# Three-block sequence model on one core: 64-row products set apart, PSUM groups copied out by ScalarE before rotation, and other moves in the order of work

## The chip, the core and the metric

The kernel runs on one core of one Trainium2 chip. The time is that of one execution on the device, in microseconds (us); lower is better. The core has five engines that run side by side and wait for one another through semaphores: TensorE (PE in the profile, with its weight loads as PEld), VectorE (DVE), ScalarE (ACT), GpSimd (POOL) and SyncE (SP), which here issues the transfers. PE writes its results to PSUM, which has eight banks of 128 rows by 512 fp32 numbers; everything else lives in SBUF.

## The reference

A sequence of 2048 tokens with 1024 channels passes through three blocks, four layers in all. Every layer projects its input with a wide matrix, mixes along the sequence in two or three branches, gates each branch, and projects back. The parts that the change touches are these:

```
# layer 1: HGRN, 4 heads of 128, chunks of 64 (beside it: sliding-window attention with rotated q and k)
G = cumsum(log_f);  q_dec = q*exp(G);  k_dec = k*exp(-G)
A = tril(q_dec @ k_dec^T)
o = A @ v + q_dec @ S_prev
S = exp(G_last)*S_prev + (k*exp(G_last-G))^T @ v

# layers 2 (gated linear attention) and 3 (retention): 4 heads, 64 key rows and 128 value columns each
scores = causal_or_decay(q @ k^T)
o = scores @ v + q @ s_in           # s_in: state entering the chunk
# layer 3: q and k are rotated first
rot(x) = concat(x1*cos - x2*sin, x1*sin + x2*cos)

# layer 4: mLSTM, 4 heads of 128; gates from two columns per head
i_pre = h @ w_i + b_i;  lf = log_sigmoid(h @ w_f + b_f)
b = cumsum(lf);  m = running max of (b_t - b_s + i_s);  decays and weights from exp of these
# every layer
mix = branch * silu(gate);   out = mix @ w_out
```

All inputs are fp32, and so is the output.

## The kernel before

The 2048 tokens are worked in four blocks of 512 (`TB`). `run` takes the blocks in pairs and goes through the layers pair by pair: layer 1 for blocks 0 and 1, layer 2 for blocks 0 and 1, and so on to layer 4, then the same for blocks 2 and 3. So each layer stands four times in the program.

**Projections.** Each fp32 operand is split into a rounded high part and the rest: `ah` and `al` for the activations, `whi` and `wlo` for the weights. A transfer on SP brings 128 x 1024 weights into `wst`, ACT casts them to `whi` (L444), DVE subtracts to get `wlo` (the L313 helper). A product then costs three matmuls of 128x512 for every 128 channels. `in_b` makes one group of 128 output channels by 512 tokens (24 matmuls into one bank); `in_b4` makes four such groups in halves at the start of a layer; `in_a` makes four token tiles by 512 channels in four banks; `out_proj` ends the layer. Four banks carry the tag `acc` (projections), four the tag `mm` (all small products). `mmul` (L322) and `tr` (L325, a transpose against `ident`) are the only lines that issue PE work; `act` is L299, `stt` L310, `tt` L313, `ts` L318. SBUF tiles come from pools: `u` has 13 buffers of 128x512, `t` 7, `g` 2.

**What sets the order.** The code is written in program order, and a list scheduler orders each engine's queue at build time by its own estimates and by priority: `hp()` puts an instruction ahead of the others, `later(n)` behind. The small products of the branches are so fed in between the matmuls of the projections. Each engine then runs its queue strictly in order.

**Layer 1.** `rope1` (called for k, and by `stack_q` for q: five groups of 512 tokens a block) rotates: DVE shuffles the PSUM group within 32 rows (L792) and multiplies the PSUM group by the cosines, both with `hp()`, then two more DVE steps. `hgrn_head` does one HGRN head: four scans (L1011), `decays` (L736 ff.: exponentials of the running sums on ACT), the products for q and k, then on PE the scores, a masked copy by DVE (L1023, L1024), the transposes of k (copied out by ACT, L759), the state increments `inc`, then `state_chain` on DVE (six small steps in a chain), the outputs and their norm. All four heads are written one after another, and behind them the four gate groups of the window branch.

**Layers 2 and 3.** `pair_heads` handles two heads at once, one in rows 0 to 63 and one in rows 64 to 127 of the same tiles. Scores: four products of 64 rows for the first head, masked, then four for the second. Then transposes, `inc` (products of 64 columns), the state chain. Then head by head: for each of the four sub-blocks a 128-row product of masked scores and values, and a 64-row product of q with the state, in turn. It is called twice a layer: sixteen times in all. In layer 3 the rotation is written out in `layer3` (shuffle L1237); it stands right behind `in_b4`, and the four banks it reads are the ones that the following `in_a` writes.

**Layer 4.** After a narrow `in_a(264)` that also yields the gate columns `ift`, the q and k projection `in_a` runs with the hook `gates_out` (transposes of `ift` at its step j = 1), then v for the attention, then v for the mLSTM with a hook that calls `qk_out` (norms of q and k, then their transposes) at step 0, `ml_gates` at step 1, and the band attention from step 2. `ml_gates` ends with two small pieces on PE, a product of `ones4` with `dd` and four transposes, whose columns `dec` and `tok` the heads read.

**Gates at the end of a layer.** `gate_mix` reads the four banks of the last `in_a`: ACT makes a tanh into a `g` buffer, DVE multiplies it with the bank again (`gate`), POOL multiplies into `mix`. The `g` pool has two buffers. `out_proj` needs those four banks next.

Of the kernel before, what the change touches and what calls it, by code (L numbers as in the profile page):

```python
# [226 lines left out]
class Build:  # L227
# [545 lines left out]
    def gate_mix(self, accs, c0, n=512, half=None):  # L773
        for t in range(4):
            g = self.g((128, n))
# [13 lines left out]
    def rope1(self, ps, out, C, S):  # L789
        sh = self.t()  # L790
        with self.hp():
            self.nc.vector.stream_shuffle(sh, ps, [i + 8 if i < 8 else (i - 8 if i < 16 else i) for i in range(32)])  # L792
            self.tt(out, ps, C, ALU.mult)
        self.tt(sh, sh, S, ALU.mult)
        self.tt(out, out, sh, ALU.add)

    def layer1(self, b, lc):
# [65 lines left out]
        for h in range(4):  # L863
            self.hgrn_head(h, kds[h], fs[h], qs[h])
        for c in range(4):
# [3 lines left out]
            self.tt(m, m, g, ALU.mult, nc.gpsimd)  # L869

# [136 lines left out]
    def hgrn_head(self, h, kd, lf, qs):  # L1007
# [6 lines left out]
        self.tt(kd, kd, eN, ALU.mult)  # L1014
        ps = self.mm()
# [153 lines left out]
    def pair_heads(self, g, qd, kd, S, em, finish, coef=None):  # L1169

        ams = []
        for i in range(2):
            r = slice(64 * i, 64 * i + 64)
            ps = self.mm()
            for t in range(4):
                c = slice(t * 128, t * 128 + 128)
                self.mmul(ps[:, c], kd[r, c], qd[r, c])
            ams.append(self.masked(ps))
# [7 lines left out]
        else:  # L1186
# [3 lines left out]
            for t in range(4):  # L1190
                c = slice(t * 128, t * 128 + 128)
                dst = Ss[:, t * 128 + 128:t * 128 + 256] if t < 3 else S
                self.stt(dst, Ss[:, c], coef, iv[:, c], ALU.mult, ALU.add)
        for i in range(2):
            r = slice(64 * i, 64 * i + 64)
            o = self.mm()
            for t in range(4):
                c = slice(t * 128, t * 128 + 128)
                self.mmul(o[:, c], ams[i][:, c], self.vb[:, t, 2 * g + i, 0:128], start=True, stop=False)
                self.mmul(o[:, c], qd[r, c], Ss[r, c], start=False, stop=True)  # L1200
            finish(o, 2 * g + i)
# [22 lines left out]
    def layer3(self, b, lc):  # L1224
# [7 lines left out]
        for i in range(4):  # L1232
# [3 lines left out]
            with self.hp():  # L1236
                nc.vector.stream_shuffle(sh, ps, perm)  # L1237
                self.tt(s, ps, C, ALU.mult)
# [65 lines left out]
    def layer4(self, b, lc):  # L1304
# [36 lines left out]
        def gates_out(j):  # L1341
            if j == 1:
# [20 lines left out]
        def qk_out(j):  # L1363
            if j != 0:
                return
# [4 lines left out]
            for t, qk in enumerate(qks):  # L1370
                qk = qk.rearrange("p (h d) -> p h d", h=8)
                self.tt(qk, qk, y[:, 8 * t:8 * t + 8].unsqueeze(2).to_broadcast([128, 8, 64]), ALU.mult)
            for g in range(4):
# [26 lines left out]
        def hook(j):  # L1400
            qk_out(j)
            if j == 1:
                gt.extend(self.ml_gates(gps[0]))
# [200 lines left out]
    def ml_gates(self, ps):  # L1604
# [39 lines left out]
        self.tt(dd.rearrange("p (h c) -> p h c", h=4), self.col("dsel", 0, 16, 0, 4).rearrange("p (h c) -> p h c", h=4), dc.unsqueeze(1).to_broadcast([4, 4, 4]), ALU.mult)  # L1644
# [106 lines left out]
```

## Time and profile before

| | |
|---|---|
| time, median of 3 runs | 3857.72 us (3853.47 to 3861.3) |
| the profiled execution | 3849.46 us, its span 3847.7 us |
| DVE busy | 2755.3 us, 72% |
| ACT busy | 1774.8 us, 46% |
| POOL busy | 586.0 us, 15% |
| matmuls into `acc` banks | 15,360 of 20,576 records on PE |
| granted TensorE clock, mean | 0.996 |

The page lists for each engine the busy time and its share of the span, then the groups of instructions by line with the idle time before them and what ended it. A matmul of full fp32 operands (the small products of the branches) leaves two records, one with rounded operands one. A timeline row has the start and the duration in us, then engine, line, operation, output and inputs, the tile (contracted rows by output rows), the shape and how often; where the engine stood idle ahead of it, the length and the releaser stand in brackets. The ends of matmuls are modelled, so the distance between two starts says what a matmul costs. In the waits, the three numbers are us in total, times, and the longest.

### The profile page before, as it was taken

How to read it: one execution, taken by the hardware profiler on the slowest of the kernel's cores; microseconds unless marked ns; L12 is line 12 of the kernel's file. 1: busy time of each engine (PE TensorE's matmuls, PEld its weight loads, DVE VectorE, ACT ScalarE, POOL GpSimd, SP SyncE). 2: the span in 40 equal slices, each digit the busy share in tenths (PEclk: the TensorE clock that was granted, in tenths of full speed). 3: DMA queues.
4: the chain of work that ended last, by engine and by line, in shares of the span. 5: the costliest groups of instructions: out<-in, count | busy, mean ns of one | idle time of the engine just before them, and what ended most of it. 6: DMA issues, size and time to landing. Idle time of an engine off the chain costs nothing.

```text
span 3847.7 us, 54577 instructions
## 1 busy us (share of the span) xinstructions
PE 3740.3 (97%) x20576; PEld 3119.7 (81%) x20576; DVE 2755.3 (72%) x5807; ACT 1774.8 (46%) x3273; POOL 586.0 (15%) x445
## 2 busy tenths in 40 slices
PE   8999999999999999999999999999999999999999
PEld 7788788878787878888787887888887878888887
DVE  7776765667666798598677767656676767985985
ACT  6547343434242454355374573434333424653552
POOL 0110112112121201100301101121131211012003
PEclk9999999999999999999999999999999999999999
DMA  3332343433343332321423332434343433223212
GB/s 128 123 126 92 111 143 119 154 109 133 131 148 120 122 109 66 126 88 66 135 81 127 121 120 77 144 130 149 115 150 113 148 115 127 77 72 131 88 61 88
DMA packets 141528, 441.09 MB, mean 115 GB/s; under 512 B 15696, under 2 KB 15824, under 8 KB 141264
## 3 DMA queue, kind: packets, MB, share of 16 engines
q1 hardware_dynamic: 141264, 437.60, 33.5%
q8 instruction: 162, 2.65, 0.3%
q14 instruction: 102, 0.84, 0.1%
HBM read 378.82 MB, written 58.72 MB: 114 GB/s over the span
## 4 chain that ended last, share of the span: by engine, by line
PE 75%; DVE 13%; ACT 4%; DMA 3%; issue 2%; POOL 2%; SPq 0%; ACTq 0%; POOLq 0%; DVEq 0%
PE acc L322 61%; PE mm L322 10%; PE mm L325 4%; DVE wlo L313 3%; DMA wst<-in_wi_dram 3%; DVE u L310 2%; DVE t L313 1%; ACT whi L444 1%; POOL mix L313 1%; ACT t L299 1%; DVE t L310 1%; POOL u L313 0%; DVE g L310 0%; DVE mix L310 0%; DVE big L310 0%
## 5 line engine op out<-in xcount | busy, mean ns | idle before, releaser
L322 PE MATMUL acc<-whi,ah 128*128 128x512 f32 (+3 forms) x3072 | 1174.9, 382 | 31.3 <-DVE g L310 15.0
L322 PE MATMUL acc<-wlo,ah 128*128 128x512 f32 (+3 forms) x3072 | 1164.1, 379 | 0.0
L322 PE MATMUL acc<-whi,al 128*128 128x512 f32 (+3 forms) x3072 | 1162.1, 378 | 0.0
L313 DVE TENSOR_TENSOR wlo<-wst,whi 128x1024 fp32r<-128x1024 f32 (+2 forms) x560 | 732.0, 1308 | 475.2 <-ACT whi L444 453.7
L444 ACT CAST whi<-wst 128x1024 fp32r<-128x1024 f32 (+2 forms) x560 | 573.9, 1025 | 965.9 <-PE acc L322 609.9
L322 PE MATMUL acc<-ah,whi 128*128 128x512 f32 (+1 forms) x2048 | 709.8, 347 | 9.1 <-ACT whi L444 9.1
L322 PEld LDWEIGHTS acc<-whi,ah 128*128 128x128 f32 x3072 | 579.3, 189 | 152.6 <-DVE g L310 23.1
L322 PE MATMUL acc<-ah,wlo 128*128 128x512 f32 (+1 forms) x2048 | 697.2, 340 | 0.5 <-DVE wlo L313 0.5
L322 PE MATMUL acc<-al,whi 128*128 128x512 f32 (+1 forms) x2048 | 697.0, 340 | 0.0
L322 PEld LDWEIGHTS acc<-whi,al 128*128 128x128 f32 x3072 | 578.9, 189 | 112.4
L322 PEld LDWEIGHTS acc<-wlo,ah 128*128 128x128 f32 x3072 | 579.9, 189 | 107.9 <-issue 1.0
L322 PEld LDWEIGHTS acc<-ah,whi 128*128 128x128 f32 x2048 | 387.1, 189 | 49.9 <-ACT whi L444 9.1
L322 PEld LDWEIGHTS acc<-ah,wlo 128*128 128x128 f32 x2048 | 386.5, 189 | 42.1 <-issue 1.4
L322 PEld LDWEIGHTS acc<-al,whi 128*128 128x128 f32 x2048 | 387.2, 189 | 41.2 <-issue 2.9
L313 POOL TENSOR_TENSOR big<-big,u 128x512 f32<-128x512 f32 x96 | 139.9, 1489 | 580.3 <-PE mm L325 236.7
L313 POOL TENSOR_TENSOR mix<-mix,g 128x512 f32<-128x512 f32 x88 | 115.5, 1324 | 588.0 <-DVE g L310 520.0
L310 DVE SCALAR_TENSOR_TENSOR u<-mix,hdw,u 128x512 f32<-128x512 f32 x240 | 170.7, 746 | 0.3
L538 ACT CAST ah<-u 128x512 fp32r<-128x512 f32 x128 | 79.2, 619 | 179.7 <-PE acc L322 167.6
L310 DVE SCALAR_TENSOR_TENSOR big<-big,acc 128x512 f32<-128x512 f32 x128 | 87.5, 683 | 77.8 <-PE acc L322 77.5
L313 POOL TENSOR_TENSOR u<-u,lc 128x512 f32<-128x512 f32 (+1 forms) x64 | 76.3, 1198 | 349.1 <-DVE u L319 172.0
L322 PE MATMUL mm<-t,u 64*128 64x128 f32 (+2 forms) x480 | 101.3, 308 | 14.5 <-DVE t L313 12.8
L310 DVE SCALAR_TENSOR_TENSOR g<-g,acc 128x512 f32<-128x512 f32 x112 | 76.0, 684 | 46.1 <-ACT g L299 46.1
(345 smaller groups left out, 4801.1 us busy)
## 6 DMA issues: line engine op xcount, KB each, us to landing
wst<-in_wi_dram SPq DMA_DIRECT2D x400, 512.0 KB, 3.3
wst<-in_wo_dram SPq DMA_DIRECT2D x128, 512.0 KB, 3.3
rows<-big SPq DMA_DIRECT2D x48, 512.0 KB, 2.7
chn<-t SPq DMA_DIRECT2D x96, 256.0 KB, 4.1
u<-chn SPq DMA_DIRECT2D x96, 256.0 KB, 4.8
big<-rows SPq DMA_DIRECT2D x48, 512.0 KB, 5.6
u<-in_lnp_dram SPq DMA_DIRECT2D x48, 256.0 KB, 5.2
u<-in_xt_dram SPq DMA_DIRECT2D x32, 256.0 KB, 4.2
```

The lines of the kernel that those rows point to most:

```text
L299: return self.nc.scalar.activation(out, in_, f, bias=bias, scale=scale)
L310: return self.nc.vector.scalar_tensor_tensor(out, in0, s, in1, op0, op1)
L313: return (eng or self.nc.vector).tensor_tensor(out, a, b, op)
L322: return self.nc.tensor.matmul(out, lhsT, rhs, start=start, stop=stop)
L325: return self.nc.tensor.transpose(out, in_, self.ident)
L444: nc.scalar.copy(hi, st)
L538: nc.scalar.copy(h, c4(st))
```

## The change

The diff has five parts.

1. `pair_heads`: both heads' scores are issued in turn, sub-block by sub-block, into two banks; the masked copies follow. At the end all eight 128-row products of both heads come first, then the eight 64-row products, the two heads in turn, into two banks at once; the norms (`finish`) follow both.
2. `gate_mix`: the third and fourth gate tile come from pool `u` in place of `g`.
3. `rope1` and `layer3`: ACT copies the PSUM group to SBUF with `hp()`. Shuffle and multiply read that copy, without `hp()`.
4. `layer4`: the transposes of `ift` are written at step 2 of the q and k projection; the norms of q and k and `ml_gates` at step 0 of the v projection, the transposes of q and k at step 1, and the PE part of the gate columns, split off as `ml_columns`, at step 2.
5. `layer1`: scans and decays of a head are split off as `hgrn_decays`. Those of heads 0 and 1 are written first; then, four times, a gate group, a head, and the decays of the head two further on.

```diff
 def gate_mix(self, accs, c0, n=512, half=None):
     for t in range(4):
-        g = self.g((128, n))
+        g = self.g((128, n)) if t < 2 else self.u((128, n))
...
 def rope1(self, ps, out, C, S):
     sh = self.t()
     with self.hp():
-        self.nc.vector.stream_shuffle(sh, ps, [i + 8 if i < 8 else (i - 8 if i < 16 else i) for i in range(32)])
-        self.tt(out, ps, C, ALU.mult)
+        self.nc.scalar.copy(out, ps)
+    self.nc.vector.stream_shuffle(sh, out, [i + 8 if i < 8 else (i - 8 if i < 16 else i) for i in range(32)])
+    self.tt(out, out, C, ALU.mult)
...
@@ layer1 @@
-        for h in range(4):
-            self.hgrn_head(h, kds[h], fs[h], qs[h])
+
+        ems = [self.hgrn_decays(h, kds[h], fs[h], qs[h]) for h in range(2)]
         for c in range(4):
             g = self.g()
             self.gate(self.in_b(), g)
             m = self.mix[:, c * 1024 + 512:c * 1024 + 1024]
             self.tt(m, m, g, ALU.mult, nc.gpsimd)
+            self.hgrn_head(c, kds[c], qs[c], ems[c])
+            if c < 2:
+                ems.append(self.hgrn_decays(c + 2, kds[c + 2], fs[c + 2], qs[c + 2]))
...
 def pair_heads(self, g, qd, kd, S, em, finish, coef=None):
-        ams = []
-        for i in range(2):
-            r = slice(64 * i, 64 * i + 64)
-            ps = self.mm()
-            for t in range(4):
-                c = slice(t * 128, t * 128 + 128)
+        rows = [slice(0, 64), slice(64, 128)]
+        pss = [self.mm() for _ in range(2)]
+        for t in range(4):
+            c = slice(t * 128, t * 128 + 128)
+            for ps, r in zip(pss, rows):
                 self.mmul(ps[:, c], kd[r, c], qd[r, c])
-            ams.append(self.masked(ps))
+        ams = [self.masked(ps) for ps in pss]
...
+        os = [self.mm() for _ in range(2)]
         for i in range(2):
-            r = slice(64 * i, 64 * i + 64)
-            o = self.mm()
             for t in range(4):
                 c = slice(t * 128, t * 128 + 128)
-                self.mmul(o[:, c], ams[i][:, c], self.vb[:, t, 2 * g + i, 0:128], start=True, stop=False)
-                self.mmul(o[:, c], qd[r, c], Ss[r, c], start=False, stop=True)
-            finish(o, 2 * g + i)
+                self.mmul(os[i][:, c], ams[i][:, c], self.vb[:, t, 2 * g + i, 0:128], start=(t == 0), stop=False)
+        for t in range(4):
+            c = slice(t * 128, t * 128 + 128)
+            for o, r in zip(os, rows):
+                self.mmul(o[:, c], qd[r, c], Ss[r, c], start=False, stop=(t == 3))
+        for i in range(2):
+            finish(os[i], 2 * g + i)
...
@@ layer3 @@
             with self.hp():
-                nc.vector.stream_shuffle(sh, ps, perm)
-                self.tt(s, ps, C, ALU.mult)
+                nc.scalar.copy(s, ps)
+            nc.vector.stream_shuffle(sh, s, perm)
+            self.tt(s, s, C, ALU.mult)
...
@@ layer4 @@
         def gates_out(j):
-            if j == 1:
+            if j == 2:
...
         def hook(j):
-            qk_out(j)
+            if j == 0:
+                qk_norm()
+                gt.extend(self.ml_gates(gps[0]))
             if j == 1:
-                gt.extend(self.ml_gates(gps[0]))
+                qk_out()
+            if j == 2:
+                gt[1:] = self.ml_columns(*gt[1:])
             if j > 1:
                 next(band)
```

What this makes of the engines' queues is shown at three places. A number behind a name tells one buffer's use from another's; the numbers of the two programs differ by what was built before.

First PE in layer 2, block 0, first pair of heads, from the state increments (`vb` with `t` in 64 columns) into the outputs; `mm_5547` and `mm_5574` are the two heads' output banks, `am0` and `am1` the masked scores, `t_5538` the states, `u_5161` q. Before:

```order
L322 MATMUL mm_5547<-vb_97,am0_114 128x128
L322 MATMUL mm_5574<-vb_97,am1_116 128x128
L322 MATMUL acc_5476<-wlo_5604,ah_94 128x512
L322 MATMUL acc_5476<-whi_5603,al_95 128x512
L322 MATMUL acc_5477<-whi_5603,ah_94 128x512
L322 MATMUL mm_5547<-t_5538,u_5161 128x128
L322 MATMUL mm_5547<-vb_97,am0_114 128x128
L322 MATMUL mm_5574<-t_5538,u_5161 128x128
L322 MATMUL mm_5574<-vb_97,am1_116 128x128
```

The same place in the changed program, with `mm_5557` and `mm_5558` for the output banks:

```order
L322 MATMUL mm_5557<-vb_97,am0_114 128x128 x4
L322 MATMUL mm_5558<-vb_97,am1_116 128x128 x4
L322 MATMUL mm_5557<-t_5548,u_5171 128x128
L322 MATMUL mm_5558<-t_5548,u_5171 128x128
L322 MATMUL acc_5486<-wlo_5614,ah_94 128x512
L322 MATMUL acc_5486<-whi_5613,al_95 128x512
L322 MATMUL acc_5487<-whi_5613,ah_94 128x512
L322 MATMUL mm_5557<-t_5548,u_5171 128x128
L322 MATMUL mm_5558<-t_5548,u_5171 128x128
```

The 128-row products now stand in one run, and behind them the 64-row ones, the two halves in turn, parted once by three matmuls of a projection.

Second, the start of layer 3, block 0. DVE before, where `acc_8673` and the following are the four banks of `in_b4`, and `wlo_9016` the weights of the v projection that comes next on PE:

```order
L313 TENSOR_TENSOR wlo_9016<-wst_9013,whi_9015 128x1024
L1237 STREAM_SHUFFLE t_8981<-acc_8673 128x512
L313 TENSOR_TENSOR u_8982<-acc_8673,lc_8412 128x512
L1237 STREAM_SHUFFLE t_8988<-acc_8731 128x512
L313 TENSOR_TENSOR u_8989<-acc_8731,lc_8412 128x512
L313 TENSOR_TENSOR wlo_9046<-wst_9043,whi_9045 128x1024
```

ACT in the changed program, where `acc_8683` and the following are those four banks:

```order
L444 CAST whi_9029<-wst_9027 128x1024
L1249 COPY u_8992<-acc_8683 128x512
L651 COPY t_8907<-mm_8902 128x512
L651 COPY t_8915<-mm_8910 128x512
L444 CAST whi_9059<-wst_9057 128x1024
L1249 COPY u_9000<-acc_8741 128x512
L444 CAST whi_9089<-wst_9087 128x1024
L1249 COPY u_9008<-acc_8789 128x512
```

The banks are freed by one ACT copy behind each cast of weights, and no longer by two DVE steps behind the subtraction of the same weights.

Third, DVE in layer 1, block 0, around the first HGRN head; `mm_1479` are its scores, `t_1463` and `t_1538` the running sums of heads 0 and 1. Before:

```order
L1011 SCALAR_TENSOR_TENSOR t_1463<-rst_111,mix_96 128x128 x4
L736 COPY sm_1468<-t_1463 128x8
L313 TENSOR_TENSOR sm_1468<-sm_1468 128x4
L313 TENSOR_TENSOR t_1471<-t_1463,sm_1468 128x512
L313 TENSOR_TENSOR wlo_1873<-wst_1870,whi_1872 128x1024
L310 SCALAR_TENSOR_TENSOR u_1424<-u_1424,acc_1425 128x512
L313 TENSOR_TENSOR u_1220<-u_1220,t_1463 128x512
L310 SCALAR_TENSOR_TENSOR u_1228<-u_1228,t_1471 128x512
L1023 COPY_PREDICATED am0_114<-cmask_103,mm_1479 64x512
L1024 COPY_PREDICATED am0_114<-cmask_103,mm_1479 64x4x64
```

In the changed program, with `t_1468` and `t_1484` for the running sums and `mm_1535` for the scores:

```order
L1015 SCALAR_TENSOR_TENSOR t_1468<-rst_111,mix_96 128x128 x4
L736 COPY sm_1473<-t_1468 128x8
L313 TENSOR_TENSOR sm_1473<-sm_1473 128x4
L313 TENSOR_TENSOR t_1476<-t_1468,sm_1473 128x512
L1015 SCALAR_TENSOR_TENSOR t_1484<-rst_111,mix_96 128x128
L313 TENSOR_TENSOR wlo_1819<-wst_1816,whi_1818 128x1024
L1015 SCALAR_TENSOR_TENSOR t_1484<-rst_111,mix_96 128x128 x3
L310 SCALAR_TENSOR_TENSOR u_1429<-u_1429,acc_1430 128x512
L313 TENSOR_TENSOR u_1225<-u_1225,t_1468 128x512
L310 SCALAR_TENSOR_TENSOR u_1233<-u_1233,t_1476 128x512
```

Head 1's scans (`t_1484`) now stand ahead of head 0's scores; before, they stood inside head 0's state chain. On PE the four heads' products, from the first scores to the last output, stretch over rows 685 to 846 of the queue with 90 projection matmuls among them, before over rows 685 to 883 with 127; the other three blocks have the same two counts.

More of the change, by code (lines that the diff above doesn't have):

```diff
@@ L1005, in swa_out, with hgrn_decays @@
             self.tt(m[r], m[r], pv[r], ALU.add)
-    def hgrn_head(self, h, kd, lf, qs):
+    def hgrn_decays(self, h, kd, lf, qs):
         nc = self.nc
@@ L1014, in hgrn_head @@
         self.tt(kd, kd, eN, ALU.mult)
+        return em
+    def hgrn_head(self, h, kd, qs, em):
+        nc = self.nc
         ps = self.mm()
@@ L1362, in layer4, with qk_norm @@
             qks.append(qk)
-        def qk_out(j):
-            if j != 0:
-                return
+        def qk_norm():
             y = self.s(32, "y32")
@@ L1372, in qk_out @@
                 self.tt(qk, qk, y[:, 8 * t:8 * t + 8].unsqueeze(2).to_broadcast([128, 8, 64]), ALU.mult)
+        def qk_out():
             for g in range(4):
@@ L1644, in ml_gates, with ml_columns @@
         self.tt(dd.rearrange("p (h c) -> p h c", h=4), self.col("dsel", 0, 16, 0, 4).rearrange("p (h c) -> p h c", h=4), dc.unsqueeze(1).to_broadcast([4, 4, 4]), ALU.mult)
+        return nM, dd, R
+    def ml_columns(self, dd, R):
+        nc = self.nc
         ps = self.mm()
@@ L1655, in ml_gates @@
         self.ts(tok[:, :, 1], tok[:, :, 1], 0.5, None, ALU.mult)
-        return nM, dec, tok
+        return dec, tok
     def ml_head(self, h, q, k, gt):
```

## The prediction

> **What bounds the kernel.** The first lines read are the engines' busy times on the page, with their shares of the span, and the chain that ended last.
>
> ```profile
> PE 3740.3 (97%) x20576; PEld 3119.7 (81%) x20576; DVE 2755.3 (72%) x5807; ACT 1774.8 (46%) x3273; POOL 586.0 (15%) x445
> PE 75%; DVE 13%; ACT 4%; DMA 3%; issue 2%; POOL 2%; SPq 0%; ACTq 0%; POOLq 0%; DVEq 0%
> ```
>
> TensorE is busy for 97% of 3847.7 us, and it leads the chain. So time is won in two ways only: PE's own work gets shorter, or one of its waits goes. Behind the page I read what PE waits for (us in total, times, longest); these are the rows that the change could touch.
>
> ```profile
> PE acc L322 <- DVE g L310: 15.0, 9, 3.9
> PE mm L322 <- DVE t L313: 14.4, 19, 1.7
> PE acc L322 <- DVE u L313: 9.9, 4, 3.6
> PE mm L325 <- DVE ift L318: 4.0, 4, 1.8
> PE mm L322 <- DVE dd L313: 3.5, 4, 0.9
> PE mm L325 <- DVE g L313: 3.0, 4, 0.8
> ```
>
> These six come to 50 us: no removal of waits can bring more than that by itself, and whatever is gained beyond must be PE work.
>
> **Part 1, `pair_heads`: PE work.** This is one pair of heads in layer 2, block 0, in PE's timeline.
>
> ```profile
> 559.80 1.71 PE L322 MATMUL mm<-u 64*128 64x128 f32 x16
> 561.44 0.66 PE L325 MATMUL mm<-ident,u 128*128 128x128 f32 x4
> ...
> 562.94 1.09 PE L322 MATMUL mm<-vb,t 128*64 128x128 f32 x16
> 563.97 0.93 PE L322 MATMUL mm<-vb,am 128*128 128x128 f32 x4
> ...
> 568.14 0.48 PE L322 MATMUL mm<-t,u 64*128 64x128 f32 x2
> 568.55 0.49 PE L322 MATMUL mm<-vb,am 128*128 128x128 f32 x2
> 568.97 0.49 PE L322 MATMUL mm<-t,u 64*128 64x128 f32 x2
> ...
> 569.80 0.49 PE L322 MATMUL mm<-t,u 64*128 64x128 f32 x4
> 570.23 0.49 PE L322 MATMUL mm<-vb,am 128*128 128x128 f32 x2
> ...
> 640.53 3.73 PE L322 MATMUL mm<-u,lc 128*128 128x128 f32 x32
> 644.02 0.47 PE L322 MATMUL acc<-whi,ah 128*128 128x512 f32 x1
> ```
>
> A fp32 product is two records. In a run of one kind it costs (644.02 - 640.53) / 16 = 0.218 us. Where 64-row and 128-row products take turns it costs 0.41 to 0.42 (568.14, 568.55, 568.97): each change between the two kinds adds about 0.197. At 569.80 stand two 64-row products behind one another, of head 0 and of head 1, so of different halves and into two banks. Both are over after 0.43 (569.80 to 570.23), as one alone is after 0.41 (568.14 to 568.55): two halves run beside one another.
>
> I counted both in the order of the two programs. Changes between a product on all rows of the array and one on half of them fall from 380 to 212: 168 x 0.197 = 33.1 us. Of the 256 products with 64 rows some 40 already follow one of the other half; in the changed order all 256 stand in turn and make 128 pairs. That is 88 more products hidden beside another, 88 x 0.218 = 19.2 us. Together -52.3.
>
> In the Trainium skill, TensorE: Matmul & The Clock Gate, Part 3 ("Measured speedup vs the span model"), four row tiles gave 3.07 times and not four; scaled to two tiles, as an estimate, 1.54 times, the second product of a pair would hide 0.153 us and not 0.218, and this part would be 6 us smaller. Against it stands the row at 562.94: eight products on alternate column halves take 1.03 us, which less one change of 0.197 is 0.21 for each pair, a full overlap.
>
> The new order also asks for something: the state products come sooner behind `inc`. The last step of DVE's chain in the same place:
>
> ```profile
> 566.51 0.56 DVE L313 TENSOR_TENSOR t<-t,em 128x384 f32<-128x384 f32 x1
> ```
>
> The state of the last three sub-blocks is ready at about 567.0, that is 3.1 us behind the end of `inc` at 563.97. In the new order PE has between them eight products (1.74), one pair and three projection matmuls with two or three changes (0.22 + 0.70 + 0.5): 3.1 to 3.2 us, less what the scores save at the start: 1.64 now (559.80 to 561.44), then four pairs and a change, 4 x 0.218 + 0.197 = 1.07. So I expect a wait of about 0.5 us in each of the eight groups of layer 2, +4. In layer 3 ACT scales the increments and the chain is shorter; nothing is put down there. The bounds of this term are 0 and 16 x 1.0. Part 1: **-48**.
>
> **Part 2, gate tiles.** Last in layer 4, two gate buffers serve four tiles: ACT stands before the third until POOL has multiplied the first (bracket of the first row), then DVE and PE follow late.
>
> ```profile
> 1558.22 0.69 ACT L299 ACTIVATE g<-acc,rs 128x512 f32<-128x512 f32 x1 [5.17 <-POOL mix L313]
> ...
> 1556.82 0.78 PE L322 MATMUL acc<-whi,ah 128*128 128x512 f32 x1 [3.89 <-DVE g L310]
> ...
> 1559.68 0.76 PE L322 MATMUL acc<-whi,ah 128*128 128x512 f32 x1
> ...
> 1865.51 0.50 PE L322 MATMUL acc<-whi,ah 128*128 128x512 f32 x1 [2.51 <-DVE g L310]
> ...
> 1868.40 0.50 PE L322 MATMUL acc<-whi,ah 128*128 128x512 f32 x1 [1.24 <-DVE g L310]
> ...
> 1869.63 0.50 PE L322 MATMUL acc<-whi,ah 128*128 128x512 f32 x1 [0.26 <-DVE g L310]
> ...
> 3792.41 0.50 PE L322 MATMUL acc<-whi,ah 128*128 128x512 f32 x1 [0.51 <-DVE g L310]
> ...
> 3796.19 0.80 PE L322 MATMUL acc<-whi,ah 128*128 128x512 f32 x1 [2.13 <-DVE g L310]
> ```
>
> The first wait of each block (1556.82, 1865.51) is for tile 0, which has its buffer: it stays. From tile 0 to tile 2 are six matmuls, to tile 3 three more, at 0.233 each (pitch below). In block 1 they took 2.89 and 1.23 where 1.40 and 0.70 would do: 2.0 us too much. In block 3, 3.78 in place of 1.40, and then a stretch at low clock (next part), 4.3 together. In blocks 0 and 2 the matmuls behind the first wait are slow anyway, and some 0.6 each goes. Sum **-7.5**; bounds 0, were another releaser as late, and -10 (the 15.0 of the row less the first waits of 3.9 and 2.5, and the low clock of 1.4).
>
> **Part 3, copies by ACT.** The start of layer 3, block 1: DVE (first two rows), then PE; the last row is the price of an ACT copy of one bank.
>
> ```profile
> 1144.86 1.23 DVE L313 TENSOR_TENSOR wlo<-wst,whi 128x1024 fp32r<-128x1024 f32 x1 [3.91 <-ACT whi L444]
> ...
> 1146.63 0.67 DVE L313 TENSOR_TENSOR u<-acc,lc 128x512 f32<-128x512 f32 x1
> ...
> 1147.45 0.77 PE L322 MATMUL acc<-whi,ah 128*128 128x512 f32 x1 [3.13 <-DVE u L313]
> ...
> 1150.57 0.45 PE L322 MATMUL acc<-wlo,ah 128*128 128x512 f32 x1
> 1150.86 0.40 PE L322 MATMUL acc<-whi,al 128*128 128x512 f32 x1
> 1151.09 0.40 PE L322 MATMUL acc<-whi,ah 128*128 128x512 f32 x1
> ...
> L784 ACT COPY vb<-acc 128x512 f32<-128x512 f32 x32 | 18.7, 586 | 17.5 <-PE acc L322 17.3
> ```
>
> The bank is freed 2.44 us behind the cast that ended at about 1144.86, by a subtraction, a shuffle and a multiplication. With the copy it is free 0.59 behind the same cast: 1.85 sooner. The row of 9.9 us has four such waits, one a block; the longest is 3.6, this one 3.1, and the other two share the rest, 1.6 each. Each loses up to 1.85: 1.85 + 1.85 + 1.6 + 1.6 = 6.9. Behind this wait seven matmuls take 3.12 us (1147.45 to 1150.57) and not 7 x 0.233 = 1.63, the latter by the pitch from 1150.86 to 1151.09; that is a low clock, worth some 1.4 us twice. Sum **-9.7**, bounds -13 and 0.
>
> Whether the shorter waits still set the clock back is not certain: above, a wait of 2.51 (1865.51) left the next matmul short at 0.50, one of 2.13 (3796.19) did not, at 0.80. The Trainium skill, TensorE: Matmul & The Clock Gate, Part 1, has the clock halved after an idle window of about 3.4 us, a window that runs freely; by that length alone neither 3.13 nor 2.13 would have done it, and the 1.4 us here and in part 2 would not be gained, 3 us less in the sum. The rows decide against the bare length.
>
> In layer 1 the q groups get one more step in a chain, where the scores of the window attention wait for them already:
>
> ```profile
> L322 PE MATMUL mm<-big,u 128*128 128x128 f32 x128 | 19.3, 284 | 5.7 <-DVE u L313 5.7
> ```
>
> The banks come free without DVE, which is busy for 72%, but the chain is longer by a copy; I take 0 between -5.7 and 20 x 0.59 = +12, since these pull opposite ways.
>
> **Part 4, gate columns.** The waits for `dd` (3.5) and for `ident,g` (3.0) have 24 or more matmuls (5.6 us) of extra cover: -6.5. The transposes of `ift` stay where they were in PE's order, since the scheduler had put them ahead, so their 4.0 stays. Bounds -6.5 and 0: **-6.5**.
>
> **Part 5, HGRN.** In each block PE waits for the state chain and what leads to it; beside the group rows, one row of a table by stretches, from 141.6 to 194.6 us (PE, PEld, DVE, ACT, POOL busy).
>
> ```profile
> L322 PE MATMUL mm<-t,u 128*128 128x128 f32 x128 | 27.5, 296 | 14.5 <-DVE t L313 12.8 <-DVE t L318 1.7
> L322 PE MATMUL mm<-u 128*64 128x128 f32 x128 | 17.4, 279 | 2.4 <-DVE u L310 2.4
> 141.60:194.60 53.00, 48.39 (x303) 38.42 (x303) 46.45 (x103) 19.95 (x51) 11.21 (x8) 1.00 0.31 102
> ```
>
> That is 16.9 us, 4.2 a block. The decays two heads ahead take DVE steps out of the chain. But between the first scores and the last output now stand 90 projection matmuls and not 127: 37 x 0.233 = 8.6 us less cover, so PE has 53.0 - 4.2 - 8.6 = 40.2 us of work beside 46.45 of DVE's, less the decays of one head that have left. Bounds: every wait goes, -17; nothing of DVE's work leaves, 46.45 - 40.2 = 6.2 of waits and not 4.2, +8. The middle, **-5**.
>
> Sum: -48 - 7.5 - 9.7 - 6.5 - 5 = -77 us, so 3849.5 becomes 3772.5. The profiled execution was 8.3 us under the median of the runs; against the median the forecast is **3781**.
>
> **Rivals.**
>
> *The halves don't run at once.* If a pair costs two products, 19.2 are missing: 3800. If each change of half also cost what a change of kind does, 14 of them in 16 groups would take 224 x 0.197 = 44 more: 3844. The row at 569.80 speaks against both.
>
> *HGRN becomes bound by DVE.* If the four heads still take 53 us, the 8.6 us of projections moved out are lost in each block: +34 in place of -5, 3820. For it speaks 46.45 of 53.0, against it that the decays of one head leave.
>
> *Only the PE work shrinks*, and the other waits return behind the next late releaser, since DVE and the transfers are 3 us nearer in each group: -48, 3810.
>
> *The other side: copies stuck behind casts.* ACT runs in order, and many casts wait until PE frees their buffer.
>
> ```profile
> ACT whi L444 <- PE acc L322: 609.9, 198, 8.4
> ```
>
> If each of the 36 copies (20 + 16) stood behind such a wait of 609.9 / 198 = 3.1 us and PE waited for its bank, that is +111 against the other parts' -67: 3901. It decides from 67 / 36 = 1.9 us a copy. Against it: the cast ahead of each layer 3 copy is of the very weights that PE needs next.
>
> **Chances.** Forecast 0.71, halves 0.05, DVE-bound 0.11, only PE work 0.10, copies 0.03. The range goes down by what parts 1, 3 and 5 may bring beyond my values (4 + 3 + 12) and the scatter of the median (8 over these runs) to 3753, and up to hold the DVE-bound case, 3822. A measurement of this kernel tells 0.2%, 7.7 us, from no change. Only the copies' rival ends slower, 0.03; of the others, mixtures of several mishaps get 0.02 within 0.2%; 0.95 are faster.
>
> **What will show it.** PE busy falls by some 50 us, and the outputs stand in runs, two 64-row products to 0.22 us. The wait for `u` L313 at layer 3 becomes a shorter one for an ACT copy; the waits of tile 2 and 3 in `gate_mix` go, `dd` goes, `ift` stays. HGRN's waits are between 0 and 6 us a block. I am wrong if 64-row pairs take over 0.3 us, or if waits for ACT copies add up beyond 10 us.

## The result, and the profile after

The changed kernel takes **3789.09 us** (median of 4 runs, 3787.27 to 3790.78); the kernel before 3856.8 on the same chip (4 runs). The ratio is 0.9824, with a 95% interval of 0.9807 to 0.9841: 1.8% faster. The forecast was 3781 in a range of 3753 to 3822. The span of the profiled execution fell from 3847.7 to 3786.2 us, by 61.5 where the sum had 77.

First the two lines of the page that answer to those of before, the busy times and the chain that ended last:

```profile
PE 3690.5 (97%) x20576; PEld 3088.3 (82%) x20576; DVE 2731.5 (72%) x5807; ACT 1785.4 (47%) x3309; POOL 589.7 (16%) x445
PE 68%; DVE 17%; ACT 6%; DMA 4%; issue 3%; POOL 1%; SPq 0%; ACTq 0%; POOLq 0%; DVEq 0%
```

PE's busy time fell by 49.8 us; the other 11.7 are waits. The kernel is still bound by PE, but DVE, ACT and DMA have a larger share of the chain. What PE waits for now:

```profile
PE mm L322 <- DVE am L1032: 11.2, 16, 1.1
...
PE mm L322 <- ACT t L759: 9.5, 6, 4.1
PE mm L322 <- DVE u L313: 8.1, 10, 3.3
...
PE acc L322 <- DVE g L310: 3.7, 4, 1.4
PE mm L325 <- DVE ift L318: 3.4, 4, 1.4
PE mm L322 <- DVE big L310: 3.2, 4, 0.8
...
PE mm L325 <- DVE big L310: 1.7, 4, 0.4
...
PE acc L322 <- ACT u L1249: 0.8, 1, 0.8
```

Against the rows of before: the waits for gates fell from 15.0 to 3.7, those for the banks of layer 3 from 9.9 to 0.8, those for `dd` and `ident,g` are gone, and HGRN's now stand at the masked scores (`am` L1032). New are 9.5 us for `t` L759, the copy of the transposed k in `pair_heads`, which stood at 0.8 before (2.2 of the 9.5 are in layer 2, 7.3 in layer 3), and 4.9 for `big` L310 in the band attention.

The same pair of heads as in the prediction, in PE's timeline (projections left out):

```profile
561.84 1.16 PE L322 MATMUL mm<-u 64*128 64x128 f32 x16
562.93 0.66 PE L325 MATMUL mm<-ident,u 128*128 128x128 f32 x4
...
566.20 2.02 PE L322 MATMUL mm<-vb,am 128*128 128x128 f32 x16 [0.41 <-DVE am L751]
568.15 0.49 PE L322 MATMUL mm<-t,u 64*128 64x128 f32 x4
...
569.49 0.94 PE L322 MATMUL mm<-t,u 64*128 64x128 f32 x12
```

The eight scores take 1.09 us from start to start (561.84 to 562.93) and took 1.64; the eight 128-row products run in 1.95 without a break, and six 64-row products stand in a row of 0.94.

For the experiments I also use a **ledger**. The order of the projection matmuls is the same in all these programs, so the time from the first projection matmul of a layer to that of the next can be compared stage by stage. Summed over the four instances of each layer, against the kernel before, in us (what is missing to the sum is the start):

| kernel | layer 1 | layer 2 | layer 3 | layer 4 | span |
|---|---|---|---|---|---|
| changed | +4.8 | -23.3 | -25.6 | -18.0 | -61.5 |
| pairs alone | -2.1 | -19.0 | -23.9 | +5.3 | -39.2 |
| gate buffers alone | +1.4 | +0.3 | -2.3 | -15.0 | -14.6 |
| layer 3 copies alone | -5.7 | +2.8 | +2.2 | +1.4 | +1.8 |
| HGRN alone | -4.5 | +3.0 | -1.5 | -1.1 | -4.1 |
| layer 1 copies alone | +5.6 | +2.6 | -1.7 | +5.3 | +12.1 |
| gate columns alone | +1.1 | +0.1 | -0.2 | -0.1 | +1.2 |
| changed, layer 3 as before | +4.6 | -21.6 | -24.4 | -16.8 | -57.1 |
| changed, halves one by one | +4.2 | -16.9 | -21.6 | -16.3 | -50.7 |
| changed, layer 1 as before | -1.8 | -19.9 | -23.1 | -17.7 | -62.9 |
| and layer 3's rotation ahead | -3.7 | -21.1 | -26.4 | -17.2 | -69.0 |
| and a third staging buffer | -8.4 | -30.1 | -37.7 | -11.2 | -87.1 |
| the same, layer 3 as before | -7.4 | -29.7 | -32.2 | -13.0 | -81.2 |

Layers that a part doesn't touch show how far single executions scatter: up to 6 us in four instances. Part of that is PE's clock, which stands at half for some stretches (last section): half of PE's busy time in these stretches is 13.2 us in the execution before, 8.2 in the changed kernel, and between 3.4 and 17.9 in the others. So a few us in this table are a hint; where a verdict rests on less, a named wait must carry it.

### The profile page after: what moved, and what is told of

Same layout as the page of the kernel before. It is cut to its first block, busy times and chain, and to the rows that moved or that the text cites. A ratio compares the mean times of both kernels' runs of the same rounds, so it can differ in the third digit from the quotient of the medians.

```text
span 3786.2 us, 54723 instructions
## 1 busy us (share of the span) xinstructions
PE 3690.5 (97%) x20576; PEld 3088.3 (82%) x20576; DVE 2731.5 (72%) x5807; ACT 1785.4 (47%) x3309; POOL 589.7 (16%) x445
## 4 chain that ended last, share of the span: by engine, by line
PE 68%; DVE 17%; ACT 6%; DMA 4%; issue 3%; POOL 1%; SPq 0%; ACTq 0%; POOLq 0%; DVEq 0%
PE acc L322 57%; PE mm L322 8%; DVE wlo L313 4%; PE mm L325 3%; DMA wst<-in_wi_dram 3%; DVE u L310 2%; ACT whi L444 2%; DVE t L313 1%; ACT t L299 1%; DVE u L313 1%; DVE big L310 1%; POOL u L313 1%; ACT mix L299 1%; DVE t L1015 0%; POOL mix L313 0%
## 5 line engine op out<-in xcount | busy, mean ns | idle before, releaser
L313 DVE TENSOR_TENSOR wlo<-wst,whi 128x1024 fp32r<-128x1024 f32 (+2 forms) x560 | 719.9, 1287 | 534.5 <-ACT whi L444 521.9
L313 POOL TENSOR_TENSOR mix<-mix,g 128x512 f32<-128x512 f32 x56 | 79.0, 1421 | 593.2 <-DVE g L310 476.9
L310 DVE SCALAR_TENSOR_TENSOR u<-mix,hdw,u 128x512 f32<-128x512 f32 x240 | 169.5, 744 | 0.1
L310 DVE SCALAR_TENSOR_TENSOR big<-big,acc 128x512 f32<-128x512 f32 x128 | 87.4, 683 | 78.3 <-PE acc L322 78.0
L322 PE MATMUL mm<-big,u 128*128 128x256 f32 (+2 forms) x616 | 96.8, 290 | 11.1 <-DVE u L313 7.1
L299 ACT ACTIVATE t<-mm,cols 128x128 f32<-128x128 f32 (+2 forms) x272 | 98.3, 488 | 15.2 <-PE mm L322 11.7
```

Of the source, the lines that this page charges most:

```text
L299: return self.nc.scalar.activation(out, in_, f, bias=bias, scale=scale)
L310: return self.nc.vector.scalar_tensor_tensor(out, in0, s, in1, op0, op1)
L313: return (eng or self.nc.vector).tensor_tensor(out, a, b, op)
L322: return self.nc.tensor.matmul(out, lhsT, rhs, start=start, stop=stop)
```

## The experiments

**Pairs alone.** The kernel before with both hunks of `pair_heads`.

```diff
...
-                self.mmul(o[:, c], ams[i][:, c], self.vb[:, t, 2 * g + i, 0:128], start=True, stop=False)
-                self.mmul(o[:, c], qd[r, c], Ss[r, c], start=False, stop=True)
+                self.mmul(os[i][:, c], ams[i][:, c], self.vb[:, t, 2 * g + i, 0:128], start=(t == 0), stop=False)
...
+            for o, r in zip(os, rows):
+                self.mmul(o[:, c], qd[r, c], Ss[r, c], start=False, stop=(t == 3))
```

> The kernel before with pair_heads alone changed. Theory (PE work, and the waits for the transposed k come from the copies of layer 3): PE busy falls by about 50 us, layers 2 and 3 each by 5.5 to 6.5 us an instance, waits for ACT t L759 stay under 2 us in all, span about 3848 - 49 = 3799. Rival (the waits for the transposed k come from the new order of pair_heads itself): waits for ACT t of 8 us or more show up here too, and the span is about 3807.

Time 3810.16, span 3808.5. The busy line of the page, and two rows of PE's waits:

```profile
PE 3692.4 (97%) x20576; PEld 3091.1 (81%) x20576; DVE 2753.0 (72%) x5807; ACT 1773.3 (47%) x3273; POOL 584.3 (15%) x445
```

```profile
PE mm L322 <- ACT t L759: 2.3, 4, 1.0
...
PE mm L322 <- DVE am L751: 1.6, 4, 0.4
```

PE's work fell by 47.9, nearly the whole 49.8 of the change, so the first half of the theory holds. The waits for the transposed k are 2.3, all in layer 2, and not 8, which is against the rival, though its span came out: layers 2 and 3 gained 43, and layer 4, which this part doesn't touch, was 5.3 longer in this execution.

**Gate buffers alone.**

```diff
-            g = self.g((128, n))
+            g = self.g((128, n)) if t < 2 else self.u((128, n))
```

> The kernel before with the gate tiles alone changed. Theory (the buffers also move the gate steps ahead of other work in DVE's queue): the first wait at the end of layer 4 shrinks from 3.9, 2.5, 3.9, 0.5 to under 1.5 us in each block, and the span falls by about 17 us to 3831. Rival (only the waits of tile 2 and 3 go, the rest comes from other parts of the change): the first waits stay, and the span falls by 7.5 us to 3840.

Time 3834.85, span 3833.1, 14.6 less than before, all of it in layer 4 (-15.0). The waits for gates are the same as in the changed kernel:

```profile
PE acc L322 <- DVE g L310: 3.7, 4, 1.4
```

The theory holds: also the first wait of each block shrank, from 3.9 to 1.4. Why is seen in DVE's timeline ahead of the gates, first of the kernel before, then of this one:

```profile
1550.83 2.17 DVE L318 TENSOR_SCALAR lc<-lc,cols 128x256 f32<-128x256 f32 x2
1552.92 2.06 DVE L313 TENSOR_TENSOR wlo<-wst,whi 128x1024 fp32r<-128x1024 f32 x1
1554.90 1.27 DVE L310 SCALAR_TENSOR_TENSOR al<-mm,ah 128x512 fp32r<-128x512 f32 x2
1556.10 1.27 DVE L310 SCALAR_TENSOR_TENSOR g<-g,acc 128x512 f32<-128x512 f32 x2
```

```profile
1552.37 0.35 DVE L318 TENSOR_SCALAR lc<-lc,cols 128x256 f32<-128x256 f32 x1
...
1552.78 1.92 DVE L313 TENSOR_TENSOR wlo<-wst,whi 128x1024 fp32r<-128x1024 f32 x1
1554.62 1.28 DVE L310 SCALAR_TENSOR_TENSOR al<-mm,ah 128x512 fp32r<-128x512 f32 x2
1555.82 1.27 DVE L310 SCALAR_TENSOR_TENSOR g<-g,acc 128x512 f32<-128x512 f32 x2
1557.01 1.27 DVE L310 SCALAR_TENSOR_TENSOR u<-u,acc 128x512 f32<-128x512 f32 x2
```

Before, two scalings of the next layer's tables stood there and took 2.17 us; here one stands there, at 0.35. With other buffers the list scheduler ordered these rows anew. POOL was at work from 1548.74 to 1553.89 in the kernel before, while the two slow scalings ran, and from 1552.53 in this one, when three of the four scalings had been done at 0.35 each. That POOL slowed them is argued from these times; no run sets it apart.

Of the 15.0, the first waits make 7.1 (10.8 before, 3.7 now), the waits of tiles 2 and 3 make 3.6, and some 3 are half clock that didn't come.

**Layer 3's copies alone.**

```diff
-                nc.vector.stream_shuffle(sh, ps, perm)
-                self.tt(s, ps, C, ALU.mult)
+                nc.scalar.copy(s, ps)
+            nc.vector.stream_shuffle(sh, s, perm)
+            self.tt(s, s, C, ALU.mult)
```

> The kernel before with the ACT copies of layer 3 alone. Theory (given back): the waits for the banks at the start of layer 3, 9.9 us, shrink to about 1, but waits for ACT t L759 of 6 to 9 us appear in pair_heads, in blocks 1 and 3 above all; span within 3 us of 3848. Rival (the copies gain what was worked out, and the new waits need the faster pair_heads): no wait for ACT t over 1 us, span about 3838.

Time 3851.62, span 3849.5; layer 3 was 2.2 longer, not 9.7 shorter. The waits for the banks went, and PE waited in `pair_heads`:

```profile
PE mm L322 <- ACT t L759: 4.8, 4, 2.6
```

That is somewhat less than the 6 to 9 expected, and 4.0 of it are in layer 3. The gain is gone all the same, and without the faster `pair_heads`. The larger part was given back behind the longest of these waits, in block 1:

```profile
1171.71 1.98 PE L322 MATMUL mm<-vb,t 128*64 128x128 f32 x16 [2.60 <-ACT t L759]
1173.62 0.80 PE L322 MATMUL mm<-vb,am 128*128 128x128 f32 x2
1174.35 0.79 PE L322 MATMUL mm<-t,u 64*128 64x128 f32 x2
```

The products of `pair_heads` stand 0.73 us apart here and 0.41 to 0.42 in the kernel before. The granted clock was 0.50 from 1171.29 to 1188.36, and over layer 3 these products took 6.5 us more, summed from start to start. So the theory holds in the waits, but in this execution the half clock behind a wait cost more than the waits did.

**The changed kernel without them**, the diff above taken back.

> The changed kernel with layer 3's rotation as before. Theory (given back): waits for ACT t L759 fall from 9.5 to under 2 us, the waits for the banks at the start of layer 3 come back with about 10 us and their low clock; span 1 to 3 us above 3786. Rival (the waits for the transposed k belong to pair_heads): they stay at 8 or more, and the span is about 3796.

Time 3792.37, span 3790.6. Two rows of PE's waits:

```profile
PE acc L322 <- DVE u L313: 9.1, 4, 3.0
...
PE mm L322 <- ACT t L759: 2.3, 4, 1.0
```

The waits change places: 0.8 and 9.5 with the copies, 9.1 and 2.3 without. Layer 3 differs by 1.2 us, the spans by 4.4. The theory holds; the 2.3 that are left are all in layer 2, as with the pairs alone. How the copy comes late is seen in the changed kernel, layer 3, block 1, by ACT, PE, DVE and SP's issues of weights:

```profile
1153.49 1.04 ACT L444 CAST whi<-wst 128x1024 fp32r<-128x1024 f32 x1 [3.58 <-DMA wst<-in_wi_dram]
1154.44 0.58 ACT L759 COPY t<-mm 128x512 f32<-128x512 f32 x1
...
1155.08 1.09 PE L322 MATMUL mm<-vb,t 128*64 128x128 f32 x16 [3.17 <-ACT t L759]
...
1149.06 2.35 DVE L313 TENSOR_TENSOR wlo<-wst,whi 128x1024 fp32r<-128x1024 f32 x2
...
1140.90 9.73 SPq L441 DMA_DIRECT2D wst<-in_wi_dram  x2
```

PE waits for the copy of the transposed k, that stands behind a cast on ACT, the cast waits for its weights, and of the two issues in SP's row the second ended at 1150.6: it had waited for a staging buffer (`wst` has two), which DVE gave back only with the subtraction that started at 1149.06.

**HGRN alone.**

```diff
+        ems = [self.hgrn_decays(h, kds[h], fs[h], qs[h]) for h in range(2)]
...
+            self.hgrn_head(c, kds[c], qs[c], ems[c])
+            if c < 2:
+                ems.append(self.hgrn_decays(c + 2, kds[c + 2], fs[c + 2], qs[c + 2]))
```

> The kernel before with the HGRN decays ahead alone. In the changed kernel layer 1 took 1.3 us more in each block, 5.3 in all. Theory (HGRN gains the 5 us of the forecast, the rotation copies lose 10): layer 1 is 1.2 to 1.5 us shorter in each block, span about 3843. Rival (HGRN itself loses what layer 1 lost, since its heads stand closer on PE): layer 1 longer by 1 to 2 us in each block, span about 3853.

Time 3845.34, span 3843.6, layer 1 4.5 shorter. Its waits:

```profile
PE mm L322 <- DVE am L1031: 11.2, 16, 1.1
```

Before, the waits for HGRN were 12.8 + 1.7 + 2.4, and 1.6 for `am`: 18.5. They fell by 7.3 and stand elsewhere, one for each of the 16 heads, at the masked scores. The theory holds in sign, so layer 1's loss came from elsewhere. The size rests on the waits: by blocks layer 1 is 0.8, 2.5, 1.0 and 0.2 shorter and not 1.2 to 1.5 each, and with layer 3's copies alone, which don't touch it, it was 5.7 shorter.

**Layer 1's copies alone.**

```diff
-            self.nc.vector.stream_shuffle(sh, ps, [i + 8 if i < 8 else (i - 8 if i < 16 else i) for i in range(32)])
-            self.tt(out, ps, C, ALU.mult)
+            self.nc.scalar.copy(out, ps)
+        self.nc.vector.stream_shuffle(sh, out, [i + 8 if i < 8 else (i - 8 if i < 16 else i) for i in range(32)])
+        self.tt(out, out, C, ALU.mult)
```

> The kernel before with the ACT copies of layer 1's rotation alone. Theory (they lengthen the chain from projection to scores): waits for u L313 before the window attention's scores grow, layer 1 longer by about 2.5 us in each block, span about 3858. Rival (layer 1's loss is HGRN's): no change beyond 1 us, span about 3848.

Time 3861.53, span 3859.8; layer 1 was 5.6 longer, of which 4.3 in block 0 and 3.0 in block 2. PE's timeline at the first scores of block 0:

```profile
52.08 0.44 PE L322 MATMUL mm<-big,u 128*128 128x128 f32 x2 [1.21 <-DVE u L313]
...
54.58 0.63 PE L322 MATMUL acc<-al,whi 128*128 128x512 f32 x1
55.01 0.63 PE L322 MATMUL acc<-ah,wlo 128*128 128x512 f32 x1
```

The scores wait 1.21 us for the rotated q, and then projections run 0.43 apart, at half their pace, for about 8 matmuls. The theory holds, in the even blocks; another 5.3 of this span are in layer 4, which the part doesn't touch. That it is the copies and not scatter is seen over all the programs: with them layer 1 of blocks 0 and 2 is 2.2 to 4.3 us longer than before (four programs), without them between 1.1 shorter and 0.8 longer (nine programs). PE's waits in layer 1 grew by 2.8 us in this run; the rest is not in the waits.

**The changed kernel without them**, the diff above taken back.

> The changed kernel with layer 1's rotation as before. Theory (the rotation copies lose there what they lost alone, 5.6 us): layer 1 about 1.4 us shorter in each block, span about 3780.5. Rival (in the changed kernel HGRN's order hides that loss): layer 1 unchanged, span 3786.

Time 3783.57 (median of 4, 3777.73 to 3788.62; ratio to before 0.9815, 0.9793 to 0.9837), span of the profiled one 3784.8. Layer 1 is 6.6 shorter than in the changed kernel (-1.8 against +4.8), again in blocks 0 and 2. The theory holds for layer 1; the median of all runs can't be told from the changed kernel's.

**Gate columns alone**, the six hunks of `layer4` and `ml_gates`.

```diff
-            if j == 1:
+            if j == 2:
                 gps.append(self.mm())
...
+            if j == 2:
+                gt[1:] = self.ml_columns(*gt[1:])
```

> The kernel before with the later gate columns alone. Theory (the waits move on): the waits for dd and for ident,g, 6.5 us, go, and waits for DVE big L310 of about 1.2 us a block come in the band attention; span 1 to 2 us shorter, 3846. Rival (the new waits have another cause): no waits for big L310, span about 3841.

Time 3850.65, span 3848.9. Three rows of PE's waits:

```profile
PE mm L325 <- DVE ift L318: 3.8, 4, 1.7
PE mm L322 <- DVE big L310: 3.2, 4, 0.8
...
PE mm L325 <- DVE big L310: 1.7, 4, 0.4
```

The waits for `dd` and `ident,g` (6.5) are gone, 4.9 of new ones have come, and layer 4 is as long as before (-0.1). The theory holds: the waits moved on. `big` L310 is the last step of the transposed k for the band attention. It belongs to `qk_out`, which the change writes a step later, behind `ml_gates`. DVE's last such step in block 0, first in the kernel before, then in this one:

```profile
1403.13 0.76 DVE L310 SCALAR_TENSOR_TENSOR big<-mm,cols,big 64x512 fp32r<-64x512 f32 x1
```

```profile
1406.55 0.76 DVE L310 SCALAR_TENSOR_TENSOR big<-mm,cols,big 64x512 fp32r<-64x512 f32 x1
```

Counted from the start of the layer it ends 2.4 us later, and PE waits for it until 1407.45.

**Halves one by one.** The changed kernel, scores and state products head by head.

```diff
...
-        for t in range(4):
-            c = slice(t * 128, t * 128 + 128)
-            for o, r in zip(os, rows):
+        for o, r in zip(os, rows):
+            for t in range(4):
+                c = slice(t * 128, t * 128 + 128)
                 self.mmul(o[:, c], qd[r, c], Ss[r, c], start=False, stop=(t == 3))
```

> The changed kernel with the 64-row products head by head, four of one half and then four of the other, scores and outputs alike; the separation from the 128-row products stays. Theory (two halves run beside one another, and the alternation is worth a product a pair): three of four pairs are lost in 32 runs, 96 x 0.218 = 21 us more, PE busy up by that, span about 3807. Rival (the gain is only the fewer changes between kinds): span within 3 us of 3786.

Time 3798.72, span 3797.0. The busy line, and the eight scores and the six 64-row products of the pair shown above:

```profile
PE 3704.8 (98%) x20576; PEld 3104.0 (82%) x20576; DVE 2733.2 (72%) x5807; ACT 1785.7 (47%) x3309; POOL 587.1 (15%) x445
```

```profile
560.90 1.71 PE L322 MATMUL mm<-u 64*128 64x128 f32 x16
562.54 0.66 PE L325 MATMUL mm<-ident,u 128*128 128x128 f32 x4
...
568.37 1.26 PE L322 MATMUL mm<-t,u 64*128 64x128 f32 x12
```

PE's work grew by 14.3 us, and the six products took 1.26 and not 0.94. The theory holds in kind and was too large in size. Counted in this program's order the scheduler left one more pair in turn in each of the 16 groups, so 80 pairs were lost and not 96, which makes 14.3 / 80 = 0.18 for each and not 0.218. The difference lies at the change of half. The eight scores take 1.64 (560.90 to 562.54), as in the kernel before; eight products at 0.218 and a change of kind would be 1.94, so 0.30 are hidden at that one change, and not the one product of 0.218 that was counted.

**Layer 3's rotation ahead**, on top of layer 1 as before.

```diff
             with self.hp():
                 nc.scalar.copy(s, ps)
-            nc.vector.stream_shuffle(sh, s, perm)
-            self.tt(s, s, C, ALU.mult)
+                nc.vector.stream_shuffle(sh, s, perm)
+                self.tt(s, s, C, ALU.mult)
```

> As the run without rotation copies in layer 1, and layer 3's shuffle and multiplication again with hp(), behind the ACT copy. Theory (the later rotation steps delay the subtraction of the weights on DVE, so a staging buffer comes free late, so the cast waits for its transfer with the copy of the transposed k behind it): waits for ACT t L759 fall from 9.5 to under 4 us, layer 3 shorter by 5 us in all, span about 3775. Rival (the copy simply stands behind a cast in ACT's queue, whatever DVE does): the waits stay at 8 or more, span unchanged within 2 us of the run without the copies of layer 1.

Time 3780.67 (median of 4; ratio 0.9811, 0.9796 to 0.9826). The row that it was for:

```profile
PE mm L322 <- ACT t L759: 9.0, 6, 3.9
```

It did not move (9.0 without this step, too), so this theory fell: the place of these DVE steps isn't what decides. The rival has the row right, the copy stands behind a cast; why that cast is late the next run shows.

**A third staging buffer**, on top of that.

```diff
-        self.wst = pool("wst", 2)
+        self.wst = pool("wst", 3)
```

> As the run with layer 3's rotation ahead, and three staging buffers for weights in place of two. Theory (transfers start late because a staging buffer is taken): casts wait less for transfers, the waits for ACT t L759 and those at the start of layer 3 all but go, span 4 to 10 us shorter than that run. Rival (the transfers themselves are the limit there, rows and weights compete): within 2 us of that run.

Time **3763.4** (median of 4, 3761.92 to 3765.05; ratio 0.9766, 0.9751 to 0.9781), 17.3 less than without it, and the fastest here. How long casts wait for transfers, first in the changed kernel, then in this one (us, times, longest):

```profile
ACT whi L444 <- DMA wst<-in_wi_dram: 158.4, 79, 5.7
```

```profile
ACT whi L444 <- DMA wst<-in_wi_dram: 28.1, 20, 2.8
```

(In the run that this one builds on it was 142.5.) No wait for `t` L759 is left. The theory holds and gained more than expected: layers 2 and 3 are 9 and 11 us shorter. The transfers were not too slow, they were issued too late. Not all of it is gain: layer 4 is 6 us longer, and a new row leads PE's waits, spread over all four layers.

```profile
PE mm L325 <- ACT big L299: 13.4, 12, 1.5
```

**The same without layer 3's copies.** Layer 3's rotation as before, three buffers.

```diff
-                nc.scalar.copy(s, ps)
-                nc.vector.stream_shuffle(sh, s, perm)
-                self.tt(s, s, C, ALU.mult)
+                nc.vector.stream_shuffle(sh, ps, perm)
+                self.tt(s, ps, C, ALU.mult)
```

> Three staging buffers for weights, layer 3's rotation and layer 1's as before, the rest of the change in. It tells what the copies of layer 3 are worth where transfers don't come late. Theory (the copies take work out of the way of the four banks, and only late transfers took the gain back): the four waits for u L313 at the start of layer 3 come back with 3 us or more in all, and layer 3 is longer than in the run with three buffers and the copies by 4 to 10 us in its four instances. Rival (the waits for the banks were late transfers too, and the copies are worth nothing once these are gone): no wait over 0.5 us at the start of layer 3, layer 3 within 1.5 us of that run.

Time 3768.65 (median of 4; ratio 0.9775, 0.9759 to 0.9791). At the start of layer 3 PE waits again:

```profile
PE acc L322 <- DVE u L313: 4.8, 4, 1.4
```

Layer 3 is 5.5 us longer than with the copies (-32.2 against -37.7). The theory holds: with weights in time the copies are worth their place.

## Why the prediction was right, and where not

The forecast was 2.0% faster, and 1.8% was measured. Most of it rests on part 1, and that held. The terms one by one:

**`pair_heads`, -48 forecast.** Alone it took 47.9 of PE's work away, against 52.3, and layers 2 and 3 became 43 shorter. Summed from start to start over the trace, the products of `pair_heads` themselves took 50.4 us less; the other matmuls of that execution took some 2.5 more. So the fewer changes and the pairs are both right: four pairs in turn take 1.09 with one change of kind, 0.22 a pair. What was mis-sized is how much the old order hid already: 0.30 at each change of half in the scores and not 0.218. The new waits came out at about 5 for the 4 forecast (47.9 less 43), but the number is luck. The wait for the state did not come: no row of PE's waits in layers 2 and 3 of that run shows it. What came in layer 2 is 1.5 more for the transposed k and 1.1 more for the masked scores; the rest is scatter and half clock.

**Gate tiles, -7.5 forecast, -15.0 measured.** The waits of tiles 2 and 3 went as worked out. The step that failed is "it stays", of the first wait (block 2 has one of 3.90 as well, at 3485.49, which the bound of -10 did not take out of the 15.0): new buffers also gave DVE's queue another order, and the first waits shrank from 3.9, 2.5 and 3.9 to at most 1.4.

**Layer 3's copies, -9.7 forecast, about -1 in the changed kernel.** The banks came free as forecast (9.9 to 0.8). What failed is that nothing was named that would be late next. Behind it stood a copy on ACT behind a cast, behind a transfer that had no buffer: 7.3 us in layer 3, where there was none before. They are two waits, 3.17 at 1155.08 and 4.12 at 3037.04, and half clock behind them cost the products of `pair_heads` 3.2 us more than with the pairs alone. The other 2.2 of the row are in layer 2 and come with `pair_heads`. The third buffer, with and without the copies, shows their worth once that is gone, 5.5 us, still short of 9.7.

**Layer 1's copies, 0 forecast, about +6 measured** (+5.6 alone, -6.6 when undone). The bound of +12 held it; the middle was not the right choice for a chain that PE waited for already. One more step in a chain with a wait at its end is paid. The stretch of low clock behind it in block 0 is no extra over the layer: one in block 1 (from 293.93 in the kernel before) is gone in that run.

**Gate columns, -6.5 forecast, about 0 measured.** Both waits went as forecast; what failed is that nothing was put down for `qk_out`, which the same hunk moves back: 4.9 us of waits for the band attention's k that were not looked for. That `ift` stays was right.

**HGRN, -5 forecast.** 7.3 us of waits went, layer 1 alone was 4.5 shorter. That PE would wait on DVE again, since the heads stand closer, was right: 11.2 us remain, 2.8 in a block.

So the total was 61.5 and not 77 because two of six terms were given back further on (8.5 and 6.5), one turned against the change (6), `pair_heads` brought 5 less, and one term gained 7.5 more: 18.5 by these sizes, 15.5 by the spans, which is within the ledger's scatter. The copies' rival, ACT's queue behind a cast, is the mechanism that ate part 3, in `pair_heads` and not at the banks where the prediction had looked, and at some 7 us of waits and not 111. The prediction's own sign of being wrong, waits for ACT copies beyond 10 us, was meant for the copies that the change adds; of these PE waits 0.8 us. With older copies that now come late (9.5 for `t` L759, 1.6 for `u` L994 in layer 1) the sum is 11.9, so the sign was right to be there and looked at the wrong copies.

## What to carry over

Where small products on all rows and on half the rows of the array take turns, put each kind in one run, and alternate the halves within the run; both showed up here in PE's own time. A wait of PE can cost more than its length, since half clock may follow it. When a wait on the critical engine is removed, follow the same queues on for ten us: the copy that is now waited for may stand behind something that was idle before. A wait for a cast that waits for a transfer may be a missing buffer, not a slow transfer; look when it was issued.

## What the runs showed of the hardware

The half pace behind a wait of PE doesn't follow from the length of that wait alone. In the run of layer 1's copies alone 1.21 us at 52.08 was followed by some 8 matmuls 0.43 us apart, while in the kernel before a wait of 2.51 at 1865.51 was followed by none. Counting stretches of four or more such matmuls, there are 7 with 40 matmuls in the kernel before, and 2 with 12 in the changed one; small products at half pace come on top.

The traces also record the granted clock. In all of them it is either 1.00 or 0.50 of full speed, and it changes on a grid: each time at 0.50 lasts 3.41 us or two, three or five times that, and starts within one trace lie whole multiples of 3.413 apart (1147.27 less 293.93 in the kernel before is 250 of them). The kernel before spent 27.3 us at 0.50, the changed one 17.1; half of the difference is 5.1, so about 5 of the 61.5 us come from there. What PE did in a stretch of that grid, and the clock in it and in the next:

| kernel | stretch, us | PE busy, us | clock | clock in the next |
|---|---|---|---|---|
| before | 1143.86 to 1147.27 | 0.45 | 1.00 | 0.50 |
| before | 1860.65 to 1864.06 | 2.35 | 1.00 | 1.00 |
| before | 1864.06 to 1867.47 | 1.65 | 1.00 | 1.00 |
| before | 3792.60 to 3796.01 | 1.46 | 1.00 | 0.50 |
| layer 1 copies alone | 50.50 to 53.91 | 1.92 | 1.00 | 0.50 |

So the wait of 2.51 is parted by a border of the grid, and the shorter one of 2.13 ahead of 3796.19 lies in one stretch. The Trainium skill, TensorE: Matmul & The Clock Gate, Part 1, speaks of a window of about 3.4 us that runs freely, and of an idle window ahead of the low clock. The traces agree with the length and the free run; the window need not be idle, as 1.46 us of work in it did not keep the clock up. Nor is PE's busy time all that counts: 1.92 us did not keep it up where 1.65 did, and with layer 3's copies alone it stayed at 0.50 for 17.07 us in which PE was busy for 16.65. In both places PE ran small products as well or for the most part; whether these count as less work is open.
